# A hybrid decoder block on one core: one subtraction a weight chunk, one accumulation step for shift and scale

## The chip, the cores and the metric

The kernel runs on one NeuronCore of a Trainium2 chip. The metric is the device time of one execution in microseconds, the median of several runs. TensorE (PE) multiplies, VectorE (DVE) and ScalarE (ACT) do the elementwise work, GpSimd (POOL) does little, and SyncE (SP) issues the weight loads.

## What is computed

One layer: a modulated RMSNorm, attention and a state space branch side by side, an output projection, then a second modulated RMSNorm and a SwiGLU feed-forward network, all in float32 for 256 tokens of width 2048. What matters for the change is the modulation and the many products with weights:

```python
c_act = jax.nn.silu(c)
mod = (c_act @ w_mod[l] + b_mod[l])[:, None, :]
sh1, sc1, g1, sh2, sc2, g2 = jnp.split(mod, 6, axis=-1)
h = rmsnorm(x, norm1_w[l]) * (1.0 + sc1) + sh1
x = x + g1 * mixer(h, ...)            # proj = h @ w_in, ..., merged @ w_out
h = rmsnorm(x, norm2_w[l]) * (1.0 + sc2) + sh2
x = x + g2 * swiglu(h, w_ffn_in[l], w_ffn_out[l])
return rmsnorm(x, final_norm_w)
```

## The kernel before

**Products in two parts.** Every weight matrix is streamed through in chunks of 512 rows by 512 columns, 1 MB each, as a tile `raw` of 128 partitions by 4 k-blocks by 512 (`load_chunk`, line 321, issued on SP's queue; three buffers, which the modulation loads `wm` of line 665 use as well). A number is used as a high part plus a low part: `split_chunk` lets ACT cast two k-blocks to the narrower type (`hi`, line 338) and DVE subtract them from the raw ones (`lo`, line 340), then the other two. Each `hi` and `lo` tile holds two k-blocks, and the pool `wsp` has four buffers of each: two chunks. There are 332 such chunks, so 664 casts and 664 subtractions, and one chunk of another kind (`dt`, line 331).

**Kinds of chunk** (`products`). A chunk of kind `cm` does 16 products with `hi` (line 356) and then 16 with `lo` (line 360). One of kind `cm1` does, for each k-block, `hi`, `hi`, `lo` (lines 388, 390, 391), 48 in all. One of kind `tm` does the same in another layout (lines 409, 410, 411), 24 in all, with the two halves of the tokens (`ci`) one after the other. The first 44 chunks are `cm1` and `tm`; w_out and w_ffn_out are `tm`; the rest are `cm`. The very last `tm` chunk is handled by halves: the first half of the tokens of the chunk before it and of its own is done first, so that only half a chunk of products lies between the chunk before the last two and the last one's first product.

**What sets the order.** The order on each engine is that in which the code issues. `Stream.run` takes a chunk, issues the split of the next one, then vector steps of waiting tasks as far as fixed costs allow, and then the chunk's products. Engines work through their queues in order. The split of chunk i+1 stands ahead of the products of chunk i, and it can write `hi` and `lo` when the products of chunk i-1 that read the same buffers are done.

**The first part.** The shift and scale of the first norm are sums over 16 blocks (`kk`) of 128 rows of w_mod, in four rounds of 512 columns. `mod_load` loads two blocks of one section (shift or scale) by one DMA of 512 KB; for each block DVE multiplies by a column of `cs` and accumulates in `sums` (lines 629, 631), one instruction of 128x512 for each section. In round 0 the blocks 11 and 15 (`ONPE`) go to PE instead: `reduce_to` (line 606) multiplies the loaded tile by the column of `cs`, with one column out. After block 11 sixteen transposes of x follow (line 469). At the end `reduce_to` with `ones` sums `sums` over the partitions, DVE makes `sc1` and `sh1`, ACT and DVE make the split activations (`split_affine`), and only then the first chunk can be multiplied. In rounds 1 to 3 the accumulations lie between the chunks of the round before.

**The later sections** (g1, sh2, sc2, g2) are made by `mod_task`, a task that the stream advances beside the chunks: a load `wm` of two blocks by 1024 columns, then four accumulations of 128x512 (line 674).

**Behind a group of columns** of w_out and of the second half of w_ffn_out, DVE multiplies and adds (lines 1215, 1216; 1355, 1356) and ACT squares the result for the next norm (lines 1217, 1358).

Of the kernel before, what the change touches and what calls it, by code (L numbers as in the profile page):

```python
# [11 lines left out]
FR = mybir.dt.float32r  # L12
AF = mybir.ActivationFunctionType
OP = mybir.AluOpType
AX = mybir.AxisListType

P = 128
D = 2048
S = 256
# [133 lines left out]
def tile_hybrid_block(  # L153
# [12 lines left out]

    const = ctx.enter_context(tc.tile_pool(name="const", bufs=1))
    wraw = ctx.enter_context(tc.tile_pool(name="wraw", bufs=3))
    wsp = ctx.enter_context(tc.tile_pool(name="wsp", bufs=4))
    slots = ctx.enter_context(tc.tile_pool(name="slots", bufs=31))  # L170
    tmp = ctx.enter_context(tc.tile_pool(name="tmp", bufs=5))
    small = ctx.enter_context(tc.tile_pool(name="small", bufs=1))
# [8 lines left out]
    def nm(s):  # L181
        uid[0] += 1
        return f"{s}{uid[0]}"

    def s4(a, b, dt=F32):
        return slots.tile([P, a, b], dt, tag="s", name=nm("s"), padded_shape=[P, a, 1024 // a])
# [74 lines left out]
                            base=0, channel_multiplier=1)  # L261


    def mod_load(sec, c0, n, kc):

        ws = []
        g = 1024 // n
        for i in range(4 // g):
            w = s4(g, n)
            r0 = kc * 512 + i * g * P  # L270
            nc.sync.dma_start(w, w_mod[r0:r0 + g * P, sec * D + c0:sec * D + c0 + n].rearrange(
                "(k p) n -> p k n", p=P))
            ws += [w[:, k, :] for k in range(g)]
        return ws

    mods = {}
    for name in ("sh1", "sc1", "g1", "sh2", "sc2", "g2"):
# [47 lines left out]
    def split_chunk(ch):  # L325
        raw = load_chunk(ch)
        got = []
        if ch["kind"] == "dt":

            for k in (0, 8):  # L330
                w = wsp.tile([P, 8, 2 * NH], FR, tag="hi", name=nm("hi"))
                A_.copy(w[:, :, :NH], raw[:, k:k + 8, :])
                V.tensor_tensor(w[:, :, NH:], raw[:, k:k + 8, :], w[:, :, :NH], op=OP.subtract)
                got += [w[:, i, :] for i in range(8)]
            return got
        for k in range(0, ch["nk"], 2):
            hi = wsp.tile([P, 2, ch["ncol"]], FR, tag="hi", name=nm("hi"), padded_shape=[P, 2, 512])
            A_.copy(hi, raw[:, k:k + 2, :])  # L338
            lo = wsp.tile([P, 2, ch["ncol"]], FR, tag="lo", name=nm("lo"), padded_shape=[P, 2, 512])
            V.tensor_tensor(lo, raw[:, k:k + 2, :], hi, op=OP.subtract)  # L340
            got += [(hi[:, i, :], lo[:, i, :]) for i in range(2)]
        return got

    def products(ch):
        if ch["accs"] is None:
# [252 lines left out]
    for r, (k0, nk) in enumerate(ROUNDS):  # L598
# [5 lines left out]
        def reduce_to(sec, w, v, stop=False):  # L604
            for j in range(nk):
                PE.matmul(cols[:, sec * 4 + j:sec * 4 + j + 1], w[:, j * P:(j + 1) * P], v,
                          start=not begun, stop=stop, skip_group_check=True)
                begun.append(1)

        nch = max(len(st.queue) - TAILCH, 0)  # L610
        if r == BIASR:
            while tk["bias"]["next"] != ("W",):
                st._force(tk["bias"])
            st._advance(tk["bias"], "W")
        for kc in range(4):
            ws = [mod_load(sec, k0 * P, nt, kc) for sec in range(2)]
            for k in range(4):
                kk = kc * 4 + k
                if r == 0 and kk in ONPE:
                    for sec in range(2):  # L620
                        reduce_to(sec, ws[sec][k], cs[:, kk:kk + 1])
                    if kk == ONPE[0]:
                        for kp in range(NEARLY, KT // 2):
                            turn_x(kp)
                    continue
                for sec in range(2):
                    d = sums[:, sec, :nt]
                    if kk == 0:
                        V.tensor_scalar(d, ws[sec][k], cs[:, kk:kk + 1], None, op0=OP.mult)
                    else:  # L630
                        V.scalar_tensor_tensor(d, ws[sec][k], cs[:, kk:kk + 1], d, op0=OP.mult, op1=OP.add)  # L631
                if k % 2:
                    m = kc * 2 + k // 2 + 1
                    while st.queue and len(st.queue) - TAILCH > nch - nch * m // 8:
                        st.run(PHASE0, len(st.queue) - 1)
        for sec in range(2):
            reduce_to(sec, sums[:, sec, :], ones[:, 0:1], True)
        V.tensor_tensor(sc1[:, k0:k0 + nk], cols[:, 4:4 + nk], bmT[:, 16 + k0:16 + k0 + nk], op=OP.add)
# [18 lines left out]
    def mod_task(secs):  # L657
        for sec, dst in secs:
            for cb in range(2):
                c0 = sec * D + cb * 1024  # L660
                a = modp.tile([P, 2, 512], F32, tag="ma", name=nm("ma"))
                for kc in range(KT // 2):
                    yield "D", 2.7, 0.0
                    w = wraw.tile([P, 4, 512], F32, tag="raw", name=nm("wm"))
                    nc.sync.dma_start(
                        w.rearrange("p (k i) n -> p k (i n)", k=2),
                        w_mod[kc * S:(kc + 1) * S, c0:c0 + 1024].rearrange("(k p) n -> p k n", p=P))
                    for k in range(2):
                        kk = kc * 2 + k
                        for i in range(2):  # L670
                            if kk == 0:
                                V.tensor_scalar(a[:, i, :], w[:, 2 * k + i, :], cs[:, kk:kk + 1], None, op0=OP.mult)
                            else:
                                V.scalar_tensor_tensor(a[:, i, :], w[:, 2 * k + i, :], cs[:, kk:kk + 1], a[:, i, :],  # L674
                                                       op0=OP.mult, op1=OP.add)
                    yield "D", 0.0, 0.0
                yield "P", 1
                ps = misc()
# [730 lines left out]
```

## Time and profile before

| | |
|---|---|
| median of three runs | 2037.5 us (2037.26 to 2038.55) |
| the profiled execution | 2037.93 us, its span 2036.2 us |
| granted TensorE clock, mean of the span | 0.995 |
| PE busy | 1989.6 us (98%) |
| DVE busy | 1484.1 us (73%), 2013 instructions |
| ACT busy | 1005.5 us (49%), 1427 instructions |
| subtractions `lo`, line 340 | 664, 791.7 us |
| casts `hi`, line 338 | 664, 667.8 us |
| accumulations, lines 631 and 674 | 116 and 240, 79.2 and 164.4 us |

Busy shares are of the whole span. Products on PE overlap, and their ends are modelled, so the distance between starts says more than the duration. An engine name with a q is its sequencer, which waits and issues. In a list of waits each row says which engine and line waited for which, the total in us, how often and the longest. In a timeline a row is one instruction, or a run of equal ones with the time from the first's start to the last's end; in brackets stands how long the engine was idle before it and what ended that.

### The profile page before, as it was taken

How to read it: one execution, taken by the hardware profiler on the slowest of the kernel's cores; microseconds unless marked ns; L12 is line 12 of the kernel's file. 1: busy time of each engine (PE TensorE's matmuls, PEld its weight loads, DVE VectorE, ACT ScalarE, POOL GpSimd, SP SyncE). 2: the span in 40 equal slices, each digit the busy share in tenths (PEclk: the TensorE clock that was granted, in tenths of full speed). 3: DMA queues.
4: the chain of work that ended last, by engine and by line, in shares of the span. 5: the costliest groups of instructions: out<-in, count | busy, mean ns of one | idle time of the engine just before them, and what ended most of it. 6: DMA issues, size and time to landing. Idle time of an engine off the chain costs nothing.

```text
span 2036.2 us, 29113 instructions
## 1 busy us (share of the span) xinstructions
PE 1989.6 (98%) x11568; PEld 1745.9 (86%) x11568; DVE 1484.1 (73%) x2013; ACT 1005.5 (49%) x1427; POOL 97.4 (5%) x176
## 2 busy tenths in 40 slices
PE   4999999999999999999999999999999999999998
PEld 4899999888888888888888888788888888888886
DVE  6788987887888888776877777777765555555564
ACT  4444335566666665554544444644444344444443
POOL 1000000001121111100000000100000000000000
PEclk8999999999999999999999999999999999999999
DMA  9988684565565666676777868586865555555553
GB/s 344 327 319 290 227 274 155 183 233 187 185 226 204 228 205 230 199 256 234 274 249 277 287 234 297 182 297 241 284 225 181 194 201 189 197 197 186 197 193 127
DMA packets 218328, 469.02 MB, mean 230 GB/s; under 512 B 10403, under 2 KB 10591, under 8 KB 218192
## 3 DMA queue, kind: packets, MB, share of 16 engines
q1 hardware_dynamic: 214080, 453.61, 64.8%
q0 software_dynamic: 4112, 13.56, 2.1%
q8 instruction: 90, 1.47, 0.3%
q14 instruction: 46, 0.38, 0.1%
HBM read 464.95 MB, written 2.18 MB: 229 GB/s over the span
## 4 chain that ended last, share of the span: by engine, by line
PE 54%; DVE 1%; DMA 1%; ACT 0%; issue 0%; ACTq 0%; DVEq 0%
PE pa L356 25%; PE pa L360 13%; PE pa L409 5%; PE pa L410 5%; PE pa L411 5%; DMA w<-in_w_ssm_proj_dram 1%; PE pb L680 0%; PE pb L699 0%; DVE lo L340 0%; DVE ma L674 0%; DVE s L1277 0%; ACT hi L338 0%; DVE s L1096 0%; DVE t L443 0%; DVE s L1150 0%
## 5 line engine op out<-in xcount | busy, mean ns | idle before, releaser
L340 DVE TENSOR_TENSOR lo<-w,hi 128x1024 fp32r<-128x1024 f32 x664 | 791.7, 1230 | 372.3 <-ACT hi L338 329.2
L338 ACT CAST hi<-w 128x1024 fp32r<-128x1024 f32 x664 | 667.8, 1048 | 555.0 <-PE pa L356 225.0
L356 PE MATMUL pa<-s,hi 128*128 128x512 f32 x3648 | 881.5, 394 | 3.1 <-DVE s L1277 1.5
L356 PEld LDWEIGHTS pa<-s,hi 128*128 128x128 f32 x3648 | 671.6, 189 | 140.9 <-issue 4.7
L360 PEld LDWEIGHTS pa<-s,lo 128*128 128x128 f32 x3648 | 467.8, 191 | 17.7
L360 PE MATMUL pa<-s,lo 128*128 128x256 f32 x3648 | 473.3, 283 | 0.0
L409 PE MATMUL pa<-hi,s 128*128 128x512 f32 x576 | 226.2, 393 | 0.0
L410 PE MATMUL pa<-lo,s 128*128 128x512 f32 x576 | 224.6, 390 | 0.7 <-DVE lo L340 0.7
L411 PE MATMUL pa<-hi,s 128*128 128x512 f32 x576 | 224.5, 390 | 0.0
L674 DVE SCALAR_TENSOR_TENSOR ma<-wm,cs,ma 128x512 f32<-128x512 f32 x240 | 164.4, 747 | 2.4 <-DMA wm<-in_w_mod_dram 2.4
L388 PE MATMUL pa<-s,hi 128*128 128x256 f32 x512 | 149.3, 292 | 3.6 <-ACT hi L338 3.6
L442 ACT COPY t<-pa 128x256 f32<-128x256 f32 x160 | 59.6, 372 | 184.2 <-PE pa L360 169.7
L391 PE MATMUL pa<-s,lo 128*128 128x256 f32 x512 | 146.8, 287 | 1.4 <-DVE lo L340 1.4
L390 PE MATMUL pa<-s,hi 128*128 128x256 f32 x512 | 146.7, 287 | 0.0
L410 PEld LDWEIGHTS pa<-lo,s 128*128 128x128 f32 x576 | 108.2, 188 | 24.2 <-DVE lo L340 1.5
L409 PEld LDWEIGHTS pa<-hi,s 128*128 128x128 f32 x576 | 108.2, 188 | 23.6 <-ACT s L494 0.6
L411 PEld LDWEIGHTS pa<-hi,s 128*128 128x128 f32 x576 | 108.2, 188 | 22.5
L388 PEld LDWEIGHTS pa<-s,hi 128*128 128x128 f32 x512 | 100.1, 195 | 6.0 <-ACT hi L338 4.4
L391 PEld LDWEIGHTS pa<-s,lo 128*128 128x128 f32 x512 | 100.0, 195 | 1.7 <-DVE lo L340 1.7
L390 PEld LDWEIGHTS pa<-s,hi 128*128 128x128 f32 x512 | 100.1, 196 | 1.0 <-issue 1.0
L443 DVE TENSOR_TENSOR s<-pa,t 128x256 f32<-128x256 f32 x128 | 53.4, 424 | 52.9 <-ACT t L442 48.5
L631 DVE SCALAR_TENSOR_TENSOR ma<-s,cs,ma 128x512 f32<-128x512 f32 x116 | 79.2, 746 | 1.8 <-DMA s<-in_w_mod_dram 1.7
(236 smaller groups left out, 1110.9 us busy)
## 6 DMA issues: line engine op xcount, KB each, us to landing
w<-in_w_in_dram SPq DMA_DIRECT2D x148, 1024.0 KB, 5.1
w<-in_w_ffn_in_dram SPq DMA_DIRECT2D x88, 1024.0 KB, 5.1
wm<-in_w_mod_dram SPq DMA_DIRECT2D x64, 1024.0 KB, 5.1
w<-in_w_ffn_out_dram SPq DMA_DIRECT2D x44, 1024.0 KB, 5.1
s<-in_w_mod_dram SPq DMA_DIRECT2D x64, 512.0 KB, 10.7
w<-in_w_ssm_proj_dram SPq DMA_DIRECT2D x32, 1024.0 KB, 5.2
w<-in_w_out_dram SPq DMA_DIRECT2D x16, 1024.0 KB, 5.3
s<-acd POOLq DMA_DIRECT2D x16, 512.0 KB, 4.7
```

What stands on the lines that cost most here:

```text
L338: A_.copy(hi, raw[:, k:k + 2, :])
L340: V.tensor_tensor(lo, raw[:, k:k + 2, :], hi, op=OP.subtract)
L356: PE.matmul(accs[n], parts[k][0][:, n * P:(n + 1) * P], act(k0 + k), start=(k0 + k == first), stop=False, skip_group_check=True)
L360: PE.matmul(accs[n][:, :S], parts[k][1][:, n * P:(n + 1) * P], act(k0 + k)[:, :S], start=False, stop=(k0 + k == last), skip_group_check=True)
L388: PE.matmul(o, w1, a[:, :S], start=(kk == first and n % 2 == 0), stop=False, skip_group_check=True)
L390: PE.matmul(o, w1, a[:, S:], start=False, stop=False, skip_group_check=True)
L391: PE.matmul(o, w2, a[:, :S], start=False, stop=(kk == last), skip_group_check=True)
L409: PE.matmul(o, xh, hi, start=(kk == first), stop=False)
L410: PE.matmul(o, xh, lo, start=False, stop=False)
L411: PE.matmul(o, xl, hi, start=False, stop=(kk == last))
L631: V.scalar_tensor_tensor(d, ws[sec][k], cs[:, kk:kk + 1], d, op0=OP.mult, op1=OP.add)
L674: V.scalar_tensor_tensor(a[:, i, :], w[:, 2 * k + i, :], cs[:, kk:kk + 1], a[:, i, :], op0=OP.mult, op1=OP.add)
```

## The change

One subtraction makes the low part of a whole chunk (128x2048), behind both casts. The tiles `hi` and `lo` hold four k-blocks, and the pool has two buffers of each, which is the same memory; a buffer is now free when the whole chunk's products are done. `mod_load` loads one block of both sections by one DMA of the same 512 KB, so that one instruction of 128x1024 accumulates shift and scale together. In `mod_task` the two halves of 1024 columns are accumulated in one instruction too. Products, casts and the number of loads stay.

```diff
-    wsp = ctx.enter_context(tc.tile_pool(name="wsp", bufs=4))
+    wsp = ctx.enter_context(tc.tile_pool(name="wsp", bufs=2))
...
-    def mod_load(sec, c0, n, kc):
-
-        ws = []
-        g = 1024 // n
-        for i in range(4 // g):
-            w = s4(g, n)
-            r0 = kc * 512 + i * g * P
-            nc.sync.dma_start(w, w_mod[r0:r0 + g * P, sec * D + c0:sec * D + c0 + n].rearrange(
-                "(k p) n -> p k n", p=P))
-            ws += [w[:, k, :] for k in range(g)]
-        return ws
+    w_mod_s = w_mod.rearrange("r (s d) -> r s d", d=D)
+
+    def mod_load(kk, c0, n):
+
+        w = s4(2, 512)[:, :, :n]
+        nc.sync.dma_start(w, w_mod_s[kk * P:(kk + 1) * P, 0:2, c0:c0 + n])
+        return w
...
-        for k in range(0, ch["nk"], 2):
-            hi = wsp.tile([P, 2, ch["ncol"]], FR, tag="hi", name=nm("hi"), padded_shape=[P, 2, 512])
-            A_.copy(hi, raw[:, k:k + 2, :])
-            lo = wsp.tile([P, 2, ch["ncol"]], FR, tag="lo", name=nm("lo"), padded_shape=[P, 2, 512])
-            V.tensor_tensor(lo, raw[:, k:k + 2, :], hi, op=OP.subtract)
-            got += [(hi[:, i, :], lo[:, i, :]) for i in range(2)]
-        return got
+        hi, lo = (wsp.tile([P, 4, ch["ncol"]], FR, tag=tag, name=nm(tag), padded_shape=[P, 4, 512])
+                  for tag in ("hi", "lo"))
+        for k in (0, 2):
+            A_.copy(hi[:, k:k + 2, :], raw[:, k:k + 2, :])
+        V.tensor_tensor(lo, raw, hi, op=OP.subtract)
+        return [(hi[:, k, :], lo[:, k, :]) for k in range(4)]
...
-        for kc in range(4):
-            ws = [mod_load(sec, k0 * P, nt, kc) for sec in range(2)]
-            for k in range(4):
-                kk = kc * 4 + k
-                if r == 0 and kk in ONPE:
-                    for sec in range(2):
-                        reduce_to(sec, ws[sec][k], cs[:, kk:kk + 1])
...
+        for kk in range(KT):
+            w = mod_load(kk, k0 * P, nt)
+            if r == 0 and kk in ONPE:
                 for sec in range(2):
...
+                    reduce_to(sec, w[:, sec, :], cs[:, kk:kk + 1])
...
+                V.scalar_tensor_tensor(sums[:, :, :nt], w, cs[:, kk:kk + 1], sums[:, :, :nt], op0=OP.mult, op1=OP.add)
...
+                        wk = w[:, 2 * k:2 * k + 2, :]
...
+                            V.scalar_tensor_tensor(a, wk, cs[:, kk:kk + 1], a, op0=OP.mult, op1=OP.add)
```

How the instructions stand before and now, at three places. First PE in round 0 of the first part, where block 11 is reduced: `s_240` and `s_244` are the tiles of its two sections, `s_239` the new tile of both; what comes ahead and behind are transposes of x. Before:

```order
L469 MATMUL pb_165<-ident,s_96 128x128
L469 MATMUL pb_165<-ident,s_100 128x128
L606 MATMUL pb_205<-cs,s_240 128x1 x4
L606 MATMUL pb_205<-cs,s_244 128x1 x4
L469 MATMUL pb_260<-ident,s_97 128x128
```

Now:

```order
L464 MATMUL pb_165<-ident,s_96 128x128
L464 MATMUL pb_165<-ident,s_100 128x128
L601 MATMUL pb_205<-cs,s_239 128x1 x8
L464 MATMUL pb_249<-ident,s_97 128x128
L464 MATMUL pb_249<-ident,s_101 128x128
```

The eight reductions stand in the same place, but all of them read one tile, where the first four read a tile of an earlier load.

SP's queue behind the 16 loads of round 0: the first weight chunk (`w58`), then modulation tiles (`s`) of round 1 and further chunks (`w`). Before:

```order
L321 DMA w58_333<-in_w_in_dram 128x4x512
L271 DMA s65_345<-in_w_mod_dram 128x2x512
L271 DMA s66_347<-in_w_mod_dram 128x2x512
L271 DMA s67_349<-in_w_mod_dram 128x2x512
L271 DMA s68_351<-in_w_mod_dram 128x2x512
L321 DMA w69_357<-in_w_in_dram 128x4x512
L321 DMA w74_419<-in_w_in_dram 128x4x512
L271 DMA s83_484<-in_w_mod_dram 128x2x512
```

Now:

```order
L317 DMA w58_319<-in_w_in_dram 128x4x512
L269 DMA s63_328<-in_w_mod_dram 128x2x512
L269 DMA s64_331<-in_w_mod_dram 128x2x512
L317 DMA w65_334<-in_w_in_dram 128x4x512
L269 DMA s68_389<-in_w_mod_dram 128x2x512
L269 DMA s69_392<-in_w_mod_dram 128x2x512
L317 DMA w70_395<-in_w_in_dram 128x4x512
L269 DMA s77_457<-in_w_mod_dram 128x2x512
```

Two modulation loads and a chunk alternate, where four and two did.

DVE at the last boundary of w_ffn_out: the multiply and add behind a group of columns, then the low parts of the next chunks, with the scaling of a finished part of the output between them. Before:

```order
L1355 TENSOR_TENSOR w2880_18038<-pa2858_17873,s2317_14505 128x512
L1356 TENSOR_TENSOR s1883_11860<-s1883_11860,w2880_18038 128x512
L340 TENSOR_TENSOR lo2883_18046<-w2881_18042,hi2882_18044 128x1024
L340 TENSOR_TENSOR lo2885_18050<-w2881_18042,hi2884_18048 128x1024
L1365 TENSOR_TENSOR s1883_11860<-s1883_11860,s2793_17493 128x1024
L340 TENSOR_TENSOR lo2890_18083<-w2888_18079,hi2889_18081 128x1024
L340 TENSOR_TENSOR lo2892_18087<-w2888_18079,hi2891_18085 128x1024
```

Now:

```order
L1344 TENSOR_TENSOR w2224_16864<-pa2210_16711,s1827_13580 128x512
L1345 TENSOR_TENSOR s1499_11132<-s1499_11132,w2224_16864 128x512
L336 TENSOR_TENSOR lo2227_16871<-w2225_16868,hi2226_16870 128x2048
L1354 TENSOR_TENSOR s1499_11132<-s1499_11132,s2167_16364 128x1024
L336 TENSOR_TENSOR lo2232_16905<-w2230_16902,hi2231_16904 128x2048
```

One subtraction stands where two did, and it reads the one tile that both casts of the chunk write.

## Rows read from the trace of the kernel before

**Rows 1.** The page's first part: each engine's busy us, share, instructions.
```profile
PE 1989.6 (98%) x11568; PEld 1745.9 (86%) x11568; DVE 1484.1 (73%) x2013; ACT 1005.5 (49%) x1427; POOL 97.4 (5%) x176
```

**Rows 2.** PE's waits: for whom, us in total, times, longest us.
```profile
PE pa L391 <- DVE lo L340: 1.4, 1, 1.4
...
PE pa L410 <- DVE lo L340: 0.7, 2, 0.4
```

**Rows 3.** DVE by line: shapes, count | busy us, mean ns | idle before.
```profile
L340 DVE TENSOR_TENSOR lo<-w,hi 128x1024 fp32r<-128x1024 f32 x664 | 791.7, 1230 | 372.3 <-ACT hi L338 329.2 <-PE pa L360 37.8 <-issue 0.3
L674 DVE SCALAR_TENSOR_TENSOR ma<-wm,cs,ma 128x512 f32<-128x512 f32 x240 | 164.4, 747 | 2.4 <-DMA wm<-in_w_mod_dram 2.4
```

**Rows 4.** Timeline of DVE at the end: start us, duration us, what.
```profile
2026.81 0.69 DVE L1355 TENSOR_TENSOR w<-pa,s 128x512 f32<-128x512 f32 x1 [1.37 <-PE pa L411]
2027.54 0.69 DVE L1356 TENSOR_TENSOR s<-s,w 128x512 f32<-128x512 f32 x1
```

**Rows 5.** Timeline of DVE, then PE, in the first 300 us.
```profile
224.29 2.36 DVE L340 TENSOR_TENSOR lo<-w,hi 128x1024 fp32r<-128x1024 f32 x2
...
227.76 2.74 DVE L631 SCALAR_TENSOR_TENSOR ma<-s,cs,ma 128x512 f32<-128x512 f32 x4
230.41 2.36 DVE L340 TENSOR_TENSOR lo<-w,hi 128x1024 fp32r<-128x1024 f32 x2
...
231.69 0.50 PE L410 MATMUL pa<-lo,s 128*128 128x512 f32 x1 [0.38 <-DVE lo L340]
```

**Rows 6.** Timeline of PE before the first chunk.
```profile
19.33 3.46 PE L469 MATMUL pb<-ident,s 128*128 128x128 f32 x15 [1.60 <-ACT s L463]
...
29.63 1.87 PE L606 MATMUL pb<-cs,s 128*128 128x1 f32 x8 [0.78 <-DMA s<-in_w_mod_dram]
31.36 3.74 PE L469 MATMUL pb<-ident,s 128*128 128x128 f32 x16
34.89 1.92 PE L606 MATMUL pb<-cs,s 128*128 128x1 f32 x16
36.67 1.93 PE L606 MATMUL pb<-ones,ma 128*128 128x1 f32 x16
```

**Rows 7.** Stretches: length, busy us by engine (count), then PEclk, DMA share, GB/s.
```profile
39.00:41.00 2.00, 0.00 (x0) 0.00 (x0) 1.24 (x4) 1.83 (x4) 0.00 (x0) 0.50 1.06 390
...
49.00:51.00 2.00, 2.00 (x19) 2.00 (x18) 2.00 (x3) 0.00 (x0) 0.00 (x0) 1.00 1.05 387
```

**Rows 8.** Timelines of DVE and PE at the first chunk.
```profile
43.13 2.35 DVE L340 TENSOR_TENSOR lo<-w,hi 128x1024 fp32r<-128x1024 f32 x2
...
44.41 0.58 PE L391 MATMUL pa<-s,lo 128*128 128x256 f32 x1 [1.38 <-DVE lo L340]
```

**Rows 9.** Timelines of ACT, DVE and PE at a boundary of w_ffn_out.
```profile
2001.06 0.63 ACT L1358 ACTIVATE w<-s 128x512 f32<-128x512 f32 x1 [2.00 <-DVE s L1356]
...
2001.69 3.10 ACT L338 CAST hi<-w 128x1024 fp32r<-128x1024 f32 x3
...
2002.76 2.36 DVE L340 TENSOR_TENSOR lo<-w,hi 128x1024 fp32r<-128x1024 f32 x2 [1.73 <-ACT hi L338]
...
2005.08 0.39 PE L410 MATMUL pa<-lo,s 128*128 128x512 f32 x1
```

**Rows 10.** Timelines of ACT and PE at a boundary of w_out.
```profile
1238.59 3.10 ACT L338 CAST hi<-w 128x1024 fp32r<-128x1024 f32 x3
...
1241.97 0.39 PE L410 MATMUL pa<-lo,s 128*128 128x512 f32 x1
```

**Rows 11.** Timelines of ACT and PE at the last chunk.
```profile
2015.93 1.06 ACT L338 CAST hi<-w 128x1024 fp32r<-128x1024 f32 x1 [0.30 <-PE pa L411]
...
2018.68 0.39 PE L410 MATMUL pa<-lo,s 128*128 128x512 f32 x1
```

**Rows 12.** Timelines of ACT and DVE before a late chunk load.
```profile
1145.37 1.98 ACT L338 CAST hi<-w 128x1024 fp32r<-128x1024 f32 x2
...
1146.84 2.35 DVE L340 TENSOR_TENSOR lo<-w,hi 128x1024 fp32r<-128x1024 f32 x2
```

More of the change, by code (lines that the diff above doesn't have):

```diff
@@ L328, in split_chunk @@
         if ch["kind"] == "dt":
-            for k in (0, 8):
-                w = wsp.tile([P, 8, 2 * NH], FR, tag="hi", name=nm("hi"))
+            for k, tag in ((0, "hi"), (8, "lo")):
+                w = wsp.tile([P, 8, 2 * NH], FR, tag=tag, name=nm("hi"), padded_shape=[P, 8, S])
                 A_.copy(w[:, :, :NH], raw[:, k:k + 8, :])
@@ L614, in tile_hybrid_block @@
             st._advance(tk["bias"], "W")
-        for kc in range(4):
-            ws = [mod_load(sec, k0 * P, nt, kc) for sec in range(2)]
-            for k in range(4):
-                kk = kc * 4 + k
-                if r == 0 and kk in ONPE:
-                    for sec in range(2):
-                        reduce_to(sec, ws[sec][k], cs[:, kk:kk + 1])
[L622 to L625, printed above, removed]
-                for sec in range(2):
[L627 to L635, printed above, removed]
+        for kk in range(KT):
+            w = mod_load(kk, k0 * P, nt)
+            if r == 0 and kk in ONPE:
+                for sec in range(2):
+                    reduce_to(sec, w[:, sec, :], cs[:, kk:kk + 1])
+                if kk == ONPE[0]:
+                    for kp in range(NEARLY, KT // 2):
+                        turn_x(kp)
+            elif kk == 0:
+                V.tensor_scalar(sums[:, :, :nt], w, cs[:, kk:kk + 1], None, op0=OP.mult)
+            else:
+                V.scalar_tensor_tensor(sums[:, :, :nt], w, cs[:, kk:kk + 1], sums[:, :, :nt], op0=OP.mult, op1=OP.add)
+            if kk % 2:
+                m = kk // 2 + 1
+                while st.queue and len(st.queue) - TAILCH > nch - nch * m // 8:
+                    st.run(PHASE0, len(st.queue) - 1)
         for sec in range(2):
@@ L669, in mod_task @@
                         kk = kc * 2 + k
[L670 to L675, printed above, removed]
+                        wk = w[:, 2 * k:2 * k + 2, :]
+                        if kk == 0:
+                            V.tensor_scalar(a, wk, cs[:, kk:kk + 1], None, op0=OP.mult)
+                        else:
+                            V.scalar_tensor_tensor(a, wk, cs[:, kk:kk + 1], a, op0=OP.mult, op1=OP.add)
                     yield "D", 0.0, 0.0
```

## The prediction

> **What bounds the kernel now.** I read the page's busy line first: PE is busy for 1989.6 us of the 2036.2 us span, DVE for 73% [rows 1]. DVE is the engine on which the change saves instructions, so the next view is what PE waits for. Over the whole run PE waits for a low part (`lo`) three times, 1.4 and 0.7 us together [rows 2]. Nearly all of the 664 subtractions are thus done before PE asks, and a cheaper one is worth nothing there. PE sets the end; the work on DVE and ACT matters only where it has little time to spare. I looked for those places in the timelines: the start, where PE idles until the first modulation columns are there; some chunks of the first 300 us; the boundaries of the two output products; and the last chunk. In each the reader is to see how long before PE's first low product the low part was ready.
>
> **Prices.** A 128x1024 subtraction takes 1.23 us, 664 times [rows 3]; a 128x512 one 0.69 us [rows 4]. The 512 further elements cost 0.54 us, so 128x2048 should take 1.23 + 1.07 = 2.30 us; I use 2.29. Two of the old ones that stand in a row take 2.36 us from the first's start to the second's end [rows 5], since the next one starts before the last has ended. One instruction for two saves DVE 0.07 us a chunk, 332 times 0.07 = 23 us, nearly all of it beside PE. The price is that PE's first low product, which needed one half (1.23 us after its cast), now needs both casts and all 2.29 us.
>
> The accumulation is the other pair: 128x512 takes 747 ns [rows 3], four in a row 2.74 us [rows 5], so 0.66 us apart. One of 128x1024 takes about 0.75 + 0.54 = 1.28 us. But the old pairs alternated between two accumulators; now each step reads what the step just before it wrote. Of two such dependent instructions the second starts 0.73 us after the first, which took 0.69 [rows 4]: 0.04 us after its end rather than 0.08 before it. Two new steps and what follows are then 1.32 + 1.20 = 2.52 us where four were 2.65: 0.13 us saved for four, not four start-up costs. Bounds: nothing, if the wait is longer, and 0.25 us, if there is none; I take 0.13.
>
> The Trainium skill (VectorE: DVE Perf Modes, "The TRN2 errata") says that the fixed cost lies between instructions, so that one large tile pays it once, and gives (N+151)/0.96 ns for an fp32 tensor_tensor: an estimate of 2291 ns for 2048 elements, which agrees with 2.29 us. By that page each removed subtraction would save 0.157 us, 52 us in all; the overlap in rows 5 leaves less than half of it.
>
> **The start.** The change loads both sections of one 128-row block by one DMA instead of two blocks of one section. Step 11 of round 0 is reduced on PE. Before, its first section's eight records ran while PE idled and the second's began at 29.63, when the DMA landed [rows 6]; that was the twelfth of 16 equal loads, and the new load of step 11 is the twelfth too. So 16 records now stand behind that landing: 29.63 + 2 x 1.73 = 33.1 us, where 31.36 was. The 16 transposes behind it took 3.53 us (31.36 to 34.89): until 36.6.
>
> Then the clock decides. The eight records at 29.63 took 1.73 us, but sixteen such took 1.78 us from 34.89 [rows 6]: PE was at the lower of its two levels until about 35 and then at the upper, after it had done transposes since 31.36. A run of 15 transposes at 19.33, 3.46 us long, was followed by slow records at 29.63 and did not raise it for good [rows 6]. By 35 us the new kernel has done less than 2 us of transposes behind one-column products, after which the clock fell to 0.50 at 39 to 41 us [rows 7]. I take it that the clock stays low: the two last groups of sixteen take 3.46 us each, 36.6 + 6.9 + 0.15 = 43.7 us against 36.67 + 1.93 = 38.6. That is **+5.1 us**. Bounds: if the clock rises at 35 all the same, the transposes end near 36.1 (with the wait for their PSUM copies), the groups take 1.78 and 1.93, and it is +1.2.
>
> All that follows waits for these columns. The first chunk's pair of subtractions began at 43.13 and PE's first low product at 44.41 [rows 8]; with one subtraction it is 43.13 + 2.29 = 45.42: **+1.0**. What clock the first chunk then meets I leave at the old length of half speed (until about 48.7, rows 7 show 1.00 from 49); bounds 0 to +1.2.
>
> The following loads alternate now: two modulation loads and a chunk, where four and two chunks stood. The first chunk loads come earlier, the later modulation loads later, each by one or two loads; as three chunk buffers let SP run ahead of DVE, I cost that at nothing. If it were not covered, a chunk of 1 MB takes 2.7 us at the 387 GB/s of rows 7.
>
> **The first 300 us.** Here DVE's own work paces chunks: two evacuations, four accumulations and two subtractions follow each other without a gap, 6.12 us a chunk (224.29 to 230.41), against 5.4 us for such a chunk on PE (24 products of 0.227 us, below), and twice PE waits, last at 231.69 for 0.38 us [rows 5]. New: 0.07 + 0.13 less, about 5.9 us. Over the nine chunks of that round 1.8 us are saved, but the whole low part is wanted 1.07 us earlier relative to its end. Of some 1.0 us of PE's delay there I expect 0.4 to stay: **-0.6**; bounds -1.0 and +1.3 (nothing saved, and the late chunk at the round's end paying 0.9).
>
> **The boundaries of the output products.** In w_out and w_ffn_out a chunk's products take high and low part in turn, so PE needs the low part one product after the chunk's start. Behind each group of columns ACT squares the result: at 2001.06, then two casts from 2001.69, together 2.0 us, the low half at 2002.76, and PE's first low product at 2005.08 [rows 9]. New: casts done at 2003.69, subtraction to 2006.03 with 0.05 us for the signal; 0.95 us late. There are three such boundaries in the second half of w_ffn_out: **+2.9**. In w_out: second cast done at 1238.59 + 2.0 = 1240.6, subtraction to 1242.9, wanted at 1241.97 [rows 10]: 1.0; the same sum gives 1.1 at 1263.7, 0.55 at 1219.7 and 0.2 at 1202.9, four places, **+2.85**. The last chunk is worse, since only half a chunk of products stands before it: casts can start when PE lets both halves go, 2015.93, so 2017.95, subtraction to 2020.3, wanted at 2018.68 [rows 11]: **+1.6**. Between boundaries PE takes 24 products of 0.227 us (60 from 2005.08 to 2018.68), 5.4 us, and casts plus subtraction 4.5: about 1 us to spare, cost nothing. Bounds for all boundaries: 4 and 9.
>
> **In the middle** the column-major chunks use the low part only after sixteen high products; the view of rows 2 has no wait of theirs (line 360) for `lo`, so I cost the later low part at nothing. One chunk load is late through its buffer: the subtraction that frees it began at 1146.84, while its second cast, from 1145.37, ends at 1147.35 [rows 12]; the new one starts after that and ends 0.5 later, and so does the load that PE waits for near 1161: **+0.5**; bounds 0 and 1.5. I add nothing for the rows of norm 2.
>
> **Sum** against the profiled execution, 2037.93 us (span 2036.2 and 1.7 around it): 5.1 + 1.0 - 0.6 + 0.5 + 2.9 + 2.85 + 1.6 = 13.4, so 2051.3; that run was 0.4 over the median, so 2051.
>
> **Rivals.**
> Clock in time: PE rises at about 35 us as before; for it, 3.5 us of transposes still run; against it, they begin 1.7 us later. Start +1.2 instead of +5.1: 2047.
> Boundaries covered: the casts find room before the squares, or the signal comes by halves. Against it: one instruction writes all of the low part, and the squares stand ahead of the casts in ACT's order. Start, first 300 us and middle alone: +6.0, 2043.5.
> More time at the lower clock: the later start or the new waits of 1 us make the clock fall or stay low once or twice more; rows 7 show ten us at 0.50 after 38.5. Another 2 to 4 us: 2054.
> DVE is the pace after all (the other side): PE's ends are modelled, and if its share hid waits for DVE, each chunk would gain 0.2 us where accumulations stand and 0.07 elsewhere. It takes 67 chunks so paced to give back 13.4 us, more than the 44 of the first 300 us; if 150 were, it is 30 us less: 2021. Against it: only the chunks of one round show DVE without a gap, and PE's waits in rows 2 are 2 us. By the page named above this saving would be largest.
> That the change does not do what it says: the new order has one 128x2048 subtraction a chunk and one 128x1024 step; not counted.
>
> **How the numbers follow.** Forecast 0.50; clock in time 0.28; more low clock 0.12; boundaries covered 0.05; DVE the pace 0.05. The range, 2045.5 to 2055, holds the first two with their bounds and most of the third. Under 0.2% (4 us, about what a measurement of this kernel can tell from no change) ends up only in the last case and at the low end of the fourth: same 0.04, faster 0.03, slower 0.93.
>
> **What would show it.** PE's last one-column group of round 0 ending near 43.7 (39.8 for the first rival), with twelve or so records in 2 us at the start of the first chunk. PE waiting for `lo` about 1 us at seven boundaries and 1.6 us at the last chunk, in its list of waits. Subtractions of 2.29 us, accumulations of 1.28 us with 0.03 between them. If PE's waits for `lo` come to under 3 us, the boundary part is wrong; if DVE steps are far longer, the prices are.

## The result, and the profile after

The changed kernel takes 2063.2 us (median, 2060.6 to 2065.8) where the kernel before, on the same chip, takes 2038.0: a ratio of 1.0124, 95% interval 1.0112 to 1.0136. It is 25 us slower. The forecast was 13.5 us slower, with a range that ended at 2055: the sign was right, and the forecast had about half of the size. The profiled execution took 2060.64 us, its span is 2058.9 us, 22.7 more than before.

The page's first part and its chain of work that ended last, of the changed kernel:

```profile
PE 1996.1 (97%) x11568; PEld 1743.5 (85%) x11568; DVE 1438.7 (70%) x1491; ACT 1001.1 (49%) x1427; POOL 94.1 (5%) x176
...
PE 45%; DVE 5%; ACT 3%; DMA 3%; issue 1%; ACTq 0%; DVEq 0%
```

DVE lost 522 instructions and 45 us of busy time [rows 1], and the kernel got slower: the saving lies on an engine that does not set the end. In the kernel before PE holds 54% of the chain and DVE 1%; now DVE, ACT and transfers have nine points more than before.

The list of PE's waits (engine and line, for whom, us in total, times, longest), changed kernel. Line 405 is the low product of a `tm` chunk (410 before), 386 that of a `cm1` chunk (391), 351 the high product of a `cm` chunk (356), 336 the subtraction (340):

```profile
PE pa L405 <- DVE lo L336: 8.3, 10, 1.7
...
PE pb L1005 <- DVE t L1002: 4.9, 3, 2.7
...
PE pa L386 <- DVE lo L336: 3.2, 2, 2.5
...
PE pa L351 <- DVE s L441: 1.6, 5, 0.6
PE pa L351 <- DVE s L1266: 1.4, 6, 0.3
PE pa L351 <- DVE s L438: 1.3, 3, 0.5
PE pb L800 <- DVE w L777: 0.7, 1, 0.7
```

Rows of the same list for the kernel before, where line 1016 is 1005 now, and 1277 and 446 are 1266 and 441:

```profile
PE pb L1016 <- DVE t L1013: 2.5, 3, 2.0
...
PE pa L356 <- DVE s L1277: 1.5, 4, 0.8
...
PE pa L356 <- DVE s L446: 0.6, 2, 0.3
```

Where [rows 2] had 2.1 us of waiting for `lo`, there are 11.5. The second row and the last four are another kind: PE waits for vector steps that have nothing to do with a low part. Together they are 9.9 us, 4.6 before. The row of line 1266 is no new one (1.4, and 1.5 before); those of 438 and 800 are new, and those of 1005 and 441 have grown.

**Where the 22.7 us arose.** Both kernels issue the same 11568 instructions on PE in the same order, so the start of any one of them can be compared in both traces. PE's first low product starts at 47.24 and started at 44.41: +2.83; the last chunk's first low product at 2041.23, and at 2018.68 before [rows 11]: +22.55. The difference at some landmarks, subtracted from landmark to landmark, gives this table (us; the stretches by the time of before; the right-hand columns are three of the experiments below):

| stretch | forecast | changed kernel | split alone | modulation alone | two subtractions |
|---|---|---|---|---|---|
| start, to the first low product | +6.1 | +2.83 | +3.71 | +4.13 | +0.92 |
| to 300 | -0.6 | +0.67 | +2.18 | -1.00 | -0.72 |
| 300 to 1150, `cm` chunks | 0 | +5.62 | +5.39 | -0.13 | +0.97 |
| 1150 to 1199, the late load | +0.5 | -0.64 | -0.53 | -0.76 | -1.16 |
| 1199 to 1286, w_out | +2.85 | +4.63 | +5.07 | +0.01 | +0.16 |
| 1286 to 1570, norm 2 and w_ffn_in | 0 | +3.06 | +3.35 | +0.01 | +0.26 |
| 1570 to the end, w_ffn_out | +4.5 | +6.52 | +6.48 | 0.00 | 0.00 |
| sum | 13.4 | 22.7 | 25.7 | 2.3 | 0.4 |

Two stretches that I had costed at nothing hold 8.7 us.

**The `cm` chunks.** Timelines of DVE, ACT and then PE in the changed kernel (start us, duration us, what, count; in brackets the idle time before and what ended it). Line 441 evacuates the accumulators of a finished group of columns, each behind a step of ACT on the same accumulator (line 440):

```profile
557.04 2.29 DVE L336 TENSOR_TENSOR lo<-w,hi 128x2048 fp32r<-128x2048 f32 x1 [1.39 <-ACT hi L335]
559.25 1.41 DVE L441 SCALAR_TENSOR_TENSOR s<-pa,t 128x256 f32<-128x256 f32 x4
...
557.87 1.18 ACT L440 ACTIVATE t<-pa 128x256 f32<-128x256 f32 x4
...
558.43 1.09 PE L351 MATMUL pa<-s,hi 128*128 128x512 f32 x4
559.72 0.50 PE L351 MATMUL pa<-s,hi 128*128 128x512 f32 x1 [0.20 <-DVE s L441]
```

DVE stands idle for 1.39 us until the second cast is done, where a first half could have been subtracted behind the first cast. So the subtraction ends late, at 559.33. The evacuation stands behind it in DVE's order and begins at 559.25, although ACT's four steps for it, 1.18 us in all, had begun at 557.87; that is 0.82 us after the next group's first product. That group's fifth product waits for the first of the four evacuations (559.25 + 0.42 = 559.67) and starts at 559.72. In the kernel before, the two halves began at 551.14 and the evacuation at 553.42, 0.29 us before the next group's start at 553.71 (DVE, then PE):

```profile
551.14 2.36 DVE L340 TENSOR_TENSOR lo<-w,hi 128x1024 fp32r<-128x1024 f32 x2 [0.43 <-ACT hi L338]
553.42 1.41 DVE L446 SCALAR_TENSOR_TENSOR s<-pa,t 128x256 f32<-128x256 f32 x4
...
553.71 2.00 PE L356 MATMUL pa<-s,hi 128*128 128x512 f32 x8
```

PE does not wait for `lo` here at all.

The largest share of the 5.62 us goes by way of a third engine. In the gated norm DVE makes a small tile (`nv`, line 289), POOL works on it in a chain of short steps (`ni`), DVE makes `t` from the result (line 1002), and PE multiplies that (line 1005). DVE, POOL, DVE and PE, changed kernel:

```profile
614.75 0.15 DVE L289 TENSOR_SCALAR nv<-pb 128x2 f32<-128x2 f32 x1
...
615.00 1.15 POOL L291 TENSOR_SCALAR ni<-nv 128x2 int32<-128x2 int32 x1 [12.54 <-DVE nv L289]
...
622.48 0.48 DVE L1002 TENSOR_SCALAR t<-ident,ni 128x128 f32<-128x128 f32 x2 [2.85 <-POOL ni L299]
...
623.02 0.48 PE L1005 MATMUL pb<-t,ones 128*128 128x256 f32 x1 [1.12 <-DVE t L1002]
```

The first of these steps stands behind a whole subtraction that began at 612.55. In the kernel before it began at 608.67; PE is 5.32 us late at this point, and this step 6.08. PE waits 1.12 us for `t` where it waited 0.24. This place and its two like (616.84, 719.82 and 878.08 us in the trace of before) cost 0.86, 0.86 and 0.70 us, 2.4 in all.

The same happens to the softmax at 320 us (DVE, then PE's transposes of its result):

```profile
320.37 2.29 DVE L336 TENSOR_TENSOR lo<-w,hi 128x2048 fp32r<-128x2048 f32 x1 [1.26 <-ACT hi L335]
...
324.69 0.55 PE L800 MATMUL pb<-ident,w 128*128 128x128 f32 x3 [0.69 <-DVE w L777]
```

and in w_ffn_in to the evacuation at line 438 (DVE, then PE), which stands behind two accumulations that stand behind the subtraction:

```profile
1367.57 2.29 DVE L336 TENSOR_TENSOR lo<-w,hi 128x2048 fp32r<-128x2048 f32 x1 [1.46 <-ACT hi L335]
1369.78 2.60 DVE L664 SCALAR_TENSOR_TENSOR ma<-wm,cs,ma 128x1024 f32<-128x1024 f32 x2
1372.29 1.41 DVE L438 TENSOR_TENSOR s<-pa,t 128x256 f32<-128x256 f32 x4
...
1372.77 0.97 PE L351 MATMUL pa<-s,hi 128*128 128x512 f32 x3 [0.54 <-DVE s L438]
```

**A boundary and the last chunk.** ACT, DVE, PE at the third boundary of w_ffn_out's second half, then at the last chunk, changed kernel, to be held against [rows 9, 11]:

```profile
2021.50 1.98 ACT L335 CAST hi<-w 128x1024 fp32r<-128x1024 f32 x2
...
2023.51 2.29 DVE L336 TENSOR_TENSOR lo<-w,hi 128x2048 fp32r<-128x2048 f32 x1 [2.67 <-ACT hi L335]
...
2025.86 0.50 PE L405 MATMUL pa<-lo,s 128*128 128x512 f32 x1 [0.94 <-DVE lo L336]
...
2036.85 2.00 ACT L335 CAST hi<-w 128x1024 fp32r<-128x1024 f32 x2 [3.44 <-PE pa L406]
...
2038.89 2.29 DVE L336 TENSOR_TENSOR lo<-w,hi 128x2048 fp32r<-128x2048 f32 x1 [3.15 <-ACT hi L335]
...
2041.23 0.50 PE L405 MATMUL pa<-lo,s 128*128 128x512 f32 x1 [1.47 <-DVE lo L336]
```

Casts, whole subtraction, product follow each other as the prediction added them up; the product is 1.10 us late here (0.95 forecast) and 1.64 at the last chunk (1.6).

### The profile page after: what moved, and what is told of

It reads as the page before. It is cut to its first block, busy times and chain, and to the rows that moved or that the text cites. A ratio compares the mean times of both kernels' runs of the same rounds, so it can differ in the third digit from the quotient of the medians.

```text
span 2058.9 us, 28185 instructions
## 1 busy us (share of the span) xinstructions
PE 1996.1 (97%) x11568; PEld 1743.5 (85%) x11568; DVE 1438.7 (70%) x1491; ACT 1001.1 (49%) x1427; POOL 94.1 (5%) x176
## 3 DMA queue, kind: packets, MB, share of 16 engines
HBM read 464.95 MB, written 2.18 MB: 227 GB/s over the span
## 4 chain that ended last, share of the span: by engine, by line
PE 45%; DVE 5%; ACT 3%; DMA 3%; issue 1%; ACTq 0%; DVEq 0%
PE pa L351 21%; PE pa L355 11%; PE pa L405 4%; PE pa L406 4%; PE pa L404 4%; DVE lo L336 3%; ACT hi L335 3%; DMA w<-in_w_ssm_proj_dram 1%; DMA w<-in_w_ffn_in_dram 1%; DMA w<-in_w_out_dram 1%; DVE ma L664 1%; PE pb L669 0%; DVE s L1266 0%; PE pb L688 0%; DMA w<-in_w_attn_proj_dram 0%
## 5 line engine op out<-in xcount | busy, mean ns | idle before, releaser
L336 DVE TENSOR_TENSOR lo<-w,hi 128x2048 fp32r<-128x2048 f32 x332 | 761.0, 2292 | 472.4 <-ACT hi L335 471.5
L664 DVE SCALAR_TENSOR_TENSOR ma<-wm,cs,ma 128x1024 f32<-128x1024 f32 x120 | 153.8, 1281 | 3.5 <-DMA wm<-in_w_mod_dram 1.2
L621 DVE SCALAR_TENSOR_TENSOR ma<-s,cs,ma 128x1024 f32<-128x1024 f32 x58 | 74.3, 1281 | 2.1 <-DMA s<-in_w_mod_dram 0.8
```

Source lines behind the costliest of these rows:

```text
L336: V.tensor_tensor(lo, raw, hi, op=OP.subtract)
L621: V.scalar_tensor_tensor(sums[:, :, :nt], w, cs[:, kk:kk + 1], sums[:, :, :nt], op0=OP.mult, op1=OP.add)
L664: V.scalar_tensor_tensor(a, wk, cs[:, kk:kk + 1], a, op0=OP.mult, op1=OP.add)
```

## The experiments

Four kernels first, to tell whether the split, the modulation or the larger buffers hold the loss.

**The split alone.**

Against the kernel before:

```diff
-    wsp = ctx.enter_context(tc.tile_pool(name="wsp", bufs=4))
+    wsp = ctx.enter_context(tc.tile_pool(name="wsp", bufs=2))
...
+        for k in (0, 2):
+            A_.copy(hi[:, k:k + 2, :], raw[:, k:k + 2, :])
+        V.tensor_tensor(lo, raw, hi, op=OP.subtract)
...
```

> Only the split of the change: one 128x2048 subtraction a chunk and two whole buffers; the modulation loads and accumulations as before. Theory G (grain): the time behind the start comes from the subtraction, which waits for both casts and cannot be passed for 2.29 us, so that PE's low products and the short vector steps queued behind it on DVE come about 1 us later; then all of the loss but the 1.73 us that the first modulation columns are late stays: 2057 to 2061 us, +19 to +23 against the kernel before, with the first low product +1.1 us after the first high one's place. Theory M (modulation): the loss that I had not priced between 300 and 1200 us and in the feed-forward product (5.1 and 3.0 us) comes from the one-step accumulations, each of which waits for the one before it; then only the first low part, the output products and the last chunk stay, 1.1 + 4.6 + 5.5 and about 1: 2048 to 2052.

Measured: 2063.4 us, ratio 1.0125 (1.0110 to 1.0140). The whole loss is there, 2.4 us above the upper end of what theory G gave. The table's column shows it in the same stretches as in the changed kernel. Its first stretch, +3.71, is not the split's alone: the loads are those of before, and yet the first chunk starts at 44.84 where the profile before has 42.23; why is told at the end of this section.

**The modulation alone.**

Against the changed kernel (the pool of four buffers too):

```diff
...
-        V.tensor_tensor(lo, raw, hi, op=OP.subtract)
...
+        for k in range(0, ch["nk"], 2):
+            hi = wsp.tile([P, 2, ch["ncol"]], FR, tag="hi", name=nm("hi"), padded_shape=[P, 2, 512])
+            A_.copy(hi, raw[:, k:k + 2, :])
+            lo = wsp.tile([P, 2, ch["ncol"]], FR, tag="lo", name=nm("lo"), padded_shape=[P, 2, 512])
+            V.tensor_tensor(lo, raw[:, k:k + 2, :], hi, op=OP.subtract)
...
```

> Only the modulation of the change: loads of both sections by one DMA and one-step accumulations; the split as before, in halves. Theory G: the 1.73 us of the start stay, and the first 300 us give back 0 to 2: 2037 to 2040.5, no group of products late between 300 us and the end. Theory M: another 8 us between 300 and 1500 us: 2046 to 2050.

Measured: 2037.4 us, ratio 1.0003 (0.9993 to 1.0012): no difference from before. Behind the first 300 us no stretch but that of the late load differs by more than 0.13 us. Theory M falls: one-step accumulations cost nothing there.

**Two subtractions in whole buffers.** Against the changed kernel:

```diff
-        V.tensor_tensor(lo, raw, hi, op=OP.subtract)
+        for k in (0, 2):
+            V.tensor_tensor(lo[:, k:k + 2, :], raw[:, k:k + 2, :], hi[:, k:k + 2, :], op=OP.subtract)
```

> The changed kernel, with its whole buffers, but each low part in two subtractions of 128x1024, each behind its own cast. Theory G: as with the modulation alone, 2037 to 2041, with PE's waits for lo back to about 2 us. Theory B (buffers): the loss comes from the whole buffers, which casts and subtractions may fill again only when PE is done with all four blocks of a chunk, where halves came free one by one; then it stays within 3 us of the changed kernel: 2058 to 2064.

Measured: 2038.6 us, ratio 1.0003 (0.9994 to 1.0013). In total the buffers cost nothing; theory B falls. PE's list of waits has one row for `lo` left:

```profile
PE pa L387 <- DVE lo L337: 0.9, 1, 0.9
```

**The same with the halves in reverse.** Against the kernel with two subtractions:

```diff
-        for k in (0, 2):
+        for k in (2, 0):
             V.tensor_tensor(lo[:, k:k + 2, :], raw[:, k:k + 2, :], hi[:, k:k + 2, :], op=OP.subtract)
```

> As the kernel with two subtractions in whole buffers, but the second half is subtracted first, so that both wait for the second cast; the work and the number of instructions are those of two subtractions. Theory G: it is the wait for the second cast and the end of the whole low part that cost, so the loss is back, with 0.07 us more a chunk where DVE paces: 2060 to 2066. If instead one long instruction as such were the cause (two short ones let something through), it stays near the kernel with two subtractions in order: 2037 to 2043.

Measured: 2067.8 us, ratio 1.0136 (1.0119 to 1.0153), from four times between 2062.4 and 2070.8. With 664 subtractions of the old length, all of the loss is back: it is not one instruction in place of two that costs, but that DVE begins behind the second cast and that the part wanted first is ready last. The median is 1.8 us above the range; in its profile w_out loses 6.2 us where the changed kernel lost 4.6, and why it is that much more stays open. That profile is not quite comparable: its granted clock is 0.946 over the span, where the other profiles of these kernels have 0.989 to 0.997. The median does not hang on that, since its three other executions, at 0.993 to 0.997, took 2062.4 to 2068.4 us.

Then each kind of chunk by itself, a mended start, and the clock at the start.

**Two subtractions for `cm` chunks alone.** Against the changed kernel:

```diff
-        V.tensor_tensor(lo, raw, hi, op=OP.subtract)
+        for k, m in (((0, 2), (2, 2)) if ch["kind"] == "cm" else ((0, 4),)):
+            V.tensor_tensor(lo[:, k:k + m, :], raw[:, k:k + m, :], hi[:, k:k + m, :], op=OP.subtract)
```

> The changed kernel, with two subtractions for the chunks of the column-major products alone (those that run all high products of a block before its low ones); the others keep one. Theory G says that these chunks lose not by PE waiting for lo but by the steps queued behind the subtraction on DVE (softmax, gated norm, evacuations, norm 2), and that it is the 5.6 us between 300 and 1150 us and the 3.1 us between 1285 and 1570 us of the changed kernel's profile: these 8.7 us go, the boundaries stay: 2063.2 - 8.7 = 2054.5, 2053 to 2056. A rival, that these waits come from the boundaries' chunks being late and are passed on, keeps them: 2061 to 2064.

Measured: 2054.2 us, ratio 1.0084 (1.0070 to 1.0097). Between 300 and 1150 us +0.98 are left of 5.62, between 1286 and 1570 us 0.02 of 3.06; w_out (4.46) and w_ffn_out (6.48) stay. At the place shown above, DVE and PE now read:

```profile
555.07 2.36 DVE L337 TENSOR_TENSOR lo<-w,hi 128x1024 fp32r<-128x1024 f32 x2 [0.44 <-ACT hi L335]
557.35 1.41 DVE L442 SCALAR_TENSOR_TENSOR s<-pa,t 128x256 f32<-128x256 f32 x4
...
557.41 3.82 PE L352 MATMUL pa<-s,hi 128*128 128x512 f32 x16
```

The evacuation begins before the next group, and that group's sixteen products run without a stop. PE's wait at the gated norm, 4.9 us in three places of the changed kernel, is 2.7 in one (before 2.5 in three). This is the step that I had costed at nothing.

**Two subtractions for `tm` chunks alone.** Against the kernel just shown:

```diff
-        for k, m in (((0, 2), (2, 2)) if ch["kind"] == "cm" else ((0, 4),)):
+        for k, m in (((0, 2), (2, 2)) if ch["kind"] == "tm" else ((0, 4),)):
             V.tensor_tensor(lo[:, k:k + m, :], raw[:, k:k + m, :], hi[:, k:k + m, :], op=OP.subtract)
```

> The changed kernel, with two subtractions for the chunks whose products take high and low part in turn in the output products and the value product; the others keep one. Theory G: the boundaries of w_out and w_ffn_out and the last chunk give back 4.6 + 1.0 + 5.5 = 11.1 us, and 0 to 0.5 us in the first 300 us: 2052, 2050.5 to 2053.5. Together with the kernel above the two savings should add up to the 23 to 24 us that two subtractions everywhere gave back, less the 1.1 to 2 us of the first chunk and its kind.

Measured: 2050.8 us, ratio 1.0067 (1.0051 to 1.0082). Now w_out and w_ffn_out show 0.00, and the `cm` stretches keep their loss (4.05 and 3.05; near 880 us, where the clock fell in the other profiles of the table, below, it did not in this one). The two savings are 0.40% and 0.57% of the time, 8.2 and 11.6 us. Together that is 19.8 of the 24.7 us that two subtractions everywhere gave back; the first chunk's 1.1 us, in neither, is part of the rest, and what remains lies within the intervals.

**A mended start.** With the modulation alone, DVE keeps pace with the loads, so a block on PE could go.

Against the kernel with the modulation alone:

```diff
-    NEARLY, ONPE = 4, (11, 15)
+    NEARLY, ONPE = 4, (10,)
```

> The split of before in halves, the modulation of the change, and at the start only one 128-row block, the eleventh, reduced on PE instead of two: DVE's one-step accumulations keep pace with the loads (1.28 us each against one load in 1.355), so that the last block needs no products of its own. PE: sixteen records from the eleventh load's landing at 28.0 us, transposes from 31.5 to 35.0, the sums from 36.1 (the last load lands at 34.73, its step takes 1.28) to 38.1. If the clock is up by then, the first chunk starts at about 41.7, 1.9 us earlier than with the modulation alone, and 0.5 us earlier than before the change; with the 0.8 us of the first 300 us and the 0.8 of the late load: 2036, 2034.5 to 2037.5. If the clock stays at its lower level, the sums take 3.46 us and the time is 2037.5 to 2039.5.

Measured: 2036.7 us, ratio 0.9996 (0.9987 to 1.0005). The sums begin at 36.28 and take 2.03 us, the first chunk starts at 41.94, much as expected, but the kernel can't be told from the one before. No kernel that I ran is shown to be faster than the one before.

**The second sixteen transposes first.** Against the changed kernel:

```diff
+                if kk == ONPE[0]:
+                    for kp in range(NEARLY, KT // 2):
+                        turn_x(kp)
                 for sec in range(2):
                     reduce_to(sec, w[:, sec, :], cs[:, kk:kk + 1])
-                if kk == ONPE[0]:
-                    for kp in range(NEARLY, KT // 2):
-                        turn_x(kp)
```

> The changed kernel with the second sixteen transposes of the start ahead of the reduced block instead of behind it, so that they run at 20.6 to 24.1 us, right behind the first. Theory C1: the clock rises with the transposes, as it did behind them in the changed kernel (37.04 us) and in before (35.05), thus early (about 22 us) and is low again when the one-column products run: sixteen at 29.45, sixteen at 34.75, the sums at 38.2 to 41.7, first chunk at 45.3 instead of 43.96: 2064 to 2067. Theory C2: the clock of the start doesn't depend on the transposes' place: the last two groups take 1.8 and 1.9 us, from 34.75 to 38.5, first chunk at 42.1: 2060.5 to 2062.

Measured: 2063.6 us, ratio 1.0131 (1.0117 to 1.0145), 0.4 us under what theory C1 gave and not to be told from the changed kernel. PE at the start, in this kernel and then in the changed one:

```profile
18.98 5.65 PE L464 MATMUL pb<-ident,s 128*128 128x128 f32 x31 [1.60 <-ACT s L458]
...
34.99 3.57 PE L601 MATMUL pb<-cs,s 128*128 128x1 f32 x16 [1.79 <-DMA s<-in_w_mod_dram]
38.43 3.55 PE L601 MATMUL pb<-ones,ma 128*128 128x1 f32 x16
45.61 0.58 PE L383 MATMUL pa<-s,hi 128*128 128x256 f32 x1 [3.63 <-ACT hi L335]
```

```profile
29.45 3.54 PE L601 MATMUL pb<-cs,s 128*128 128x1 f32 x16 [6.82 <-DMA s<-in_w_mod_dram]
32.85 3.74 PE L464 MATMUL pb<-ident,s 128*128 128x128 f32 x16
36.38 2.16 PE L601 MATMUL pb<-cs,s 128*128 128x1 f32 x16
38.41 1.93 PE L601 MATMUL pb<-ones,ma 128*128 128x1 f32 x16
43.96 0.58 PE L383 MATMUL pa<-s,hi 128*128 128x256 f32 x1 [3.63 <-ACT hi L335]
```

Thirty-one transposes in a row, and the clock rises during them: fifteen alone took 3.46 us [rows 6], thirty-one take 5.65. Both last groups of sixteen then run at the lower level, as theory C1 had it, and the first chunk starts at 45.61, 1.65 us later. But the modulation alone, whose start is that of the changed kernel, had these two groups at 3.41 and 3.55 us, and the kernel with two subtractions at 1.84 and 2.02: the level seemed to differ from execution to execution, so that this one execution can't show C1. So both kernels were profiled twice more, unchanged.

> The kernel before, unchanged, looked at once more for the clock at its start. Theory S (scatter): where the clock rises at the start differs between executions of one program: early (about 22 us, behind the first fifteen transposes, and then low until about 52), late (35 to 37 us, behind the second sixteen), or both; the group of the sums then ends near 42 or near 38.6, and the first low product starts at 44.4 or near 47.3, the execution being 3 us longer. Theory D (the change): in the kernel before the rise is always at about 35 us and the groups behind the transposes take 1.8 and 1.9 us.

> The same kernel again: a second sample for the same question. Theory S: either pattern; theory D: rise at 35 us.

> The changed kernel, unchanged, looked at once more for the clock at its start. Theory S: early rise (near 23 us) with the sums ending near 43 to 43.5 and the first low product near 50 in one or more of the looks, late rise (37 us, sums' end 40.3, first low product 47.2) in others. Theory D: the rise is at 37 us each time, as in the first profile.

> The same changed kernel again: a second sample. Theory S: either pattern; theory D: rise at 37 us.

Measured: 2038.4 and 2037.7 us (before), 2060.4 and 2060.3 (changed). The last two groups before the first chunk, in the first of the two new executions of the kernel before:

```profile
34.83 3.41 PE L606 MATMUL pb<-cs,s 128*128 128x1 f32 x16
38.10 3.55 PE L606 MATMUL pb<-ones,ma 128*128 128x1 f32 x16
45.28 0.58 PE L388 MATMUL pa<-s,hi 128*128 128x256 f32 x1 [3.63 <-ACT hi L338]
```

Here they take 3.41 and 3.55 us where [rows 6] have 1.92 and 1.93, and the first chunk starts at 45.28 instead of 42.23; in the second at 44.94. In the changed kernel's two it starts at 43.92 and 44.10, beside 43.96 in the profile above. Theory S holds for the kernel before; the changed kernel itself showed only the faster pattern in its three executions, and its start code both (43.58 with two subtractions, 46.79 with the modulation alone).

## Why the prediction went wrong

**Prices of instructions: right.** Groups of the changed kernel by line (shapes, count, busy us, mean ns, idle before):

```profile
L336 DVE TENSOR_TENSOR lo<-w,hi 128x2048 fp32r<-128x2048 f32 x332 | 761.0, 2292 | 472.4 <-ACT hi L335 471.5
...
L664 DVE SCALAR_TENSOR_TENSOR ma<-wm,cs,ma 128x1024 f32<-128x1024 f32 x120 | 153.8, 1281 | 3.5 <-DMA wm<-in_w_mod_dram 1.2
```

2.29 and 1.28 us, as worked out. The idle time in the first row says what the price list does not: DVE stood idle for 472 us ahead of subtractions, nearly all of it for casts, 372 in [rows 3].

The Trainium skill (VectorE: DVE Perf Modes, "The TRN2 errata") gives 2291 ns by its formula, and the trace agrees with 2292. Its remark that one large tile pays the fixed cost once holds for DVE's busy time in direction (30.7 us less on this line, where the prediction worked out 52 from the page); the time of the kernel went the other way.

**The start, forecast +5.1: the term was read from a single execution.** The two levels and what they cost are as predicted (16 one-column records in 3.5 or 1.9 us). What failed is the step "I take it that the clock stays low", as if the kernel before always had it high at that point: in two of its three executions it was low. Over all of them the first chunk starts at 42.23, 45.28 or 44.94 before and at 43.92 to 44.10 with the change, which shows no cost. Held pattern against pattern there is one: where the last groups are fast, 42.23 before against 43.58 to 44.10 with the new start code; where they are slow, 44.84 (the split alone), 44.94 and 45.28 with the old one against 46.79 and 46.81 (the modulation alone, and two subtractions for `tm` chunks). That is 1.4 to 2.0 us either way, about what the 16 records behind the load's landing explain: the transposes begin 1.5 us later (32.85, and 31.36 before). No pair of like patterns shows the other 3.3 us of the forecast, the clock's. The rival "clock in time" describes the profiled execution (the last group ended at 40.34, where it said 39.8). The 1.1 us of the **first chunk's low part** (forecast 1.0) is in every profiled execution of the two kernels: a wait of 2.48 us where [rows 8] had 1.38 (1.36 to 1.38 in all three), and gone with two subtractions.

**The first 300 us, -0.6 against +0.67: within its bounds, on the wrong side.** The modulation alone gave back 1.00 between the first low product and 300 us, but not as nine times 0.13: 0.83 of it came at the two chunks where PE waited in [rows 5] (0.49 and 0.34). The kernel before, unchanged, moved by -0.92 and -0.57 over the same stretch in its two new executions, there at places where the clock's level differs (near 49 and from 103 to 107 us). The low part as a whole took more than it gave, 0.89 of it at the late chunk at the round's end, which stood in the bound.

**The `cm` chunks, forecast 0, measured 5.6 + 3.1: the step that failed.** The prediction says "the view of rows 2 has no wait of theirs (line 360) for `lo`, so I cost the later low part at nothing", and for norm 2 "I add nothing". PE indeed never waits for `lo` there. But the subtraction is also a place in DVE's order. It holds DVE idle until the second cast is done, and the evacuations, softmax steps and norm steps behind it come later, one of them through POOL. The rule for an added wait, to name what is queued behind the waiting instruction and who waits for that, I had applied to the boundaries and not here. That two subtractions for these chunks take 8 us away shows it.

**The boundaries and the last chunk, 7.35 forecast.** The three of w_ffn_out and the last chunk were right within 0.2 us each. Of the rest, w_out measured 4.6 against 2.85. ACT, DVE and PE at 1253 us:

```profile
1248.64 1.98 ACT L335 CAST hi<-w 128x1024 fp32r<-128x1024 f32 x2
...
1250.65 2.29 DVE L336 TENSOR_TENSOR lo<-w,hi 128x2048 fp32r<-128x2048 f32 x1 [2.68 <-ACT hi L335]
...
1253.00 0.50 PE L405 MATMUL pa<-lo,s 128*128 128x512 f32 x1 [1.23 <-DVE lo L336]
```

PE is 1.39 us late, so it wanted the low part at 1251.61, 2.97 us after the casts began; in [rows 10] that distance is 3.38. The casts start 0.41 us later because the multiply and add ahead of the square stood behind the previous chunk's subtraction: the same step missed once more. Two smaller boundaries in w_ffn_out, near 1592 and 1946 us, which the forecast did not have, cost 1.0 together. All this lies above the upper bound of 9: 4.6 + 6.5 = 11.1.

**The late load, +0.5 against -0.64.** It came out as a gain, and with the modulation alone too (-0.76); in the two new executions of the kernel before the same place moved by -0.50 and -0.66, so the gain is not shown to be the change's.

**DVE the pace, and no gain:** rightly given little.

## What to carry to other kernels

Before two instructions on an in-order engine are merged, list what stands behind them there: the merged one starts when the last of its inputs is ready, and every step behind it, however unrelated, inherits that wait. A list of waits that shows nobody waiting for the merged result is no evidence that a later result is free. A term read at the start of one execution, where the clock decides, needs a second execution before it goes into a sum.

## What the runs showed of the hardware

The granted clock at the start is not a property of the program alone: the same sixteen one-column records took 1.92 us in one execution of the kernel before and 3.41 in another. Nor are its later falls. Stretches of 3 us of the kernel before, in the profile shown ahead and at the same place in the first of its two new executions, which is 2 us later there (length, busy us of PE, PEld, DVE, ACT, POOL with counts, PEclk, DMA share, GB/s):

```profile
878.50:881.50 3.00, 3.00 (x8) 2.33 (x8) 2.19 (x2) 0.00 (x0) 0.00 (x0) 0.50 0.31 124
```

```profile
880.00:883.00 3.00, 2.85 (x13) 2.39 (x14) 2.21 (x3) 0.00 (x0) 0.00 (x0) 1.00 0.48 194
```

PEclk is 0.50 (the lower level) in the one and 1.00 in the other, behind the same wait of PE at line 1016; 8 and 13 products begin (the second stretch starts some 0.6 us earlier in the order of instructions). Between 700 and 900 us the new execution gained 1.65 us on the old one, and with another 1.5 between 100 and 220 us, where the old one has 0.50 too (from 103.3 us), most of its 3 us late start was gone by the end: spans of 2036.7 and 2036.2. Differences of 2 or 3 us between single executions of this kernel mean nothing, and the times scatter by about as much.
